# Six latent heads' roots in pairs: one 16-column chain per even/odd pair, and side work offered at each even query tile

## The chip, the cores and the metric

One core of one Trainium2 chip runs the whole program as a single launch. The metric is the device time of that launch in microseconds (us); the time of a kernel is the median over its runs.

## The reference, cut to what matters

The program is a two-layer encoder trunk over 512 tokens of width 1024. In each layer three groups of heads read one normalised input: six latent-attention heads (A), six dilated-window heads (B) and a state-space group (C). Their outputs are normalised, concatenated, projected and added to the stream; a gated, convolved MLP follows. The change touches group A alone:

```
q = split_heads(rmsnorm(c_q, q_gain) @ w_uq, MLA_HEADS)            # 6 heads of 96
kv = split_heads(rmsnorm(c_kv, kv_gain) @ w_ukv, MLA_HEADS)
k_nope, v = jnp.split(kv, [MLA_NOPE], axis=-1)
q = rmsnorm(q, qk_gain[0])
k = rmsnorm(jnp.concatenate([k_nope, k_rope], axis=-1), qk_gain[1])
```

followed by rotary embedding and dense attention over all 512 keys, in blocks of 128 queries. What matters here are the two root-mean-square norms per head and token: one reciprocal root for each query row and one for each key row.

## The kernel before, in words

Everything is held transposed: features on partitions, 512 tokens along the free axis. Large products run as three fp32r matmuls (high part by high, low by high, high by low: `mm3`, lines 381 to 383). `mixing(l, ...)` is one layer's attention half. Its attention stage is a loop over six turns, `TURNS = (b,0) (b,1) (a,0) (b,2) (a,1) (a,2)`, each a pair of heads of group B or A. A turn has two halves of two query tiles; each query tile has one `unit` per head of the pair:

- the scores (line 1170 for B, `mm3` for A) into one of three `sc` banks;
- on VectorE (DVE) line 1117, which scales them, takes the row minimum and writes `P`. For an A head the scale is a column of `qs`, the root of the query row;
- on ScalarE (ACT) line 1119, the exponential with row sums;
- four transposes of `P` on TensorE (PE), line 1123, and a copy out on DVE or ACT (1127, 1129).

After each half, `pv` (line 1141, 16 matmuls) adds the half's part of the output. `finish_pair` at the end of a turn takes the reciprocals of the sums (`rc`, line 1149), spreads them through `bx` (411) and four transposes (415), copies the result to `rb` (1152) and multiplies (1153).

The next heads are made beside the units, by the generator `side(n)`, stepped once after each half. It calls `next_qk(h)` and so `mla_qk(h, wq)` for head 0 at the end of turn 0, head 1 in turn 1, heads 2, 3, 4 and 5 in turns 2, 3, 3 and 4. An even call also makes the raw keys of heads h and h+1 (`kps`, `kraw[0]`, `kraw[1]`). Each call appends `roots` to the list `later`:

- `roots` of an even head sums squares by matmul into `ssh` (lines 1202, 1204), 12 columns: 4 for its queries, 8 for the keys of both heads. Two DVE operations finish `hv` (1206, 1207); `rsqrt` (lines 389 to 398, nine DVE operations, each reading the one before) takes the roots; then `qs` (1210) and `rks` (1213), the key roots of both heads.
- `roots` of an odd head does the same for the 4 query columns of its own.
- Each `roots` appends a `rest`: `bcast4` (four PE transposes, line 405) spreads the key roots, DVE line 1219 multiplies the raw key into `kf`, a tile named `glg` that has one buffer, and `qk_parts` splits it with a cast on ACT (913) and a subtraction on GpSimd (POOL, 914). The same `glg` is a scratch tile of the B heads' rotary step (922, 923).

`catch_up()` runs what stands in `later` at that moment; what it appends waits for the next call. It is called after `pv` of each half, after the step of `side`, and at the end of a turn. The order of each engine's instructions is fixed when the program is built, from program order, dependences and the offsets in `PRI` (`cu` 10, `qk` 20, `fin` 20 stand later; `glu` earlier). Each engine then runs its own list strictly in order. Of eight PSUM banks in this stage three hold scores, two transposes, one `pv`, and two (`ps`) everything else: `qps`, `kps`, `ssh`, the broadcasts, the GLU and value products, in turn.

Of the kernel before, what the change touches and what calls it, by code (L numbers as in the profile page):

```python
# [29 lines left out]
SETS = {("b", 0): 0, ("b", 1): 1, ("b", 2): 0, ("a", 0): 2, ("a", 1): 3, ("a", 2): 1, ("a", 3): 2, ("a", 4): 3, ("a", 5): 0}  # L30
# [194 lines left out]
def program(ctx, tc, a, out):  # L225
    nc = tc.nc
    V, S, T, G = nc.vector, nc.scalar, nc.tensor, nc.gpsimd
    mul, add, sub, mx_, mn_ = ALU.mult, ALU.add, ALU.subtract, ALU.max, ALU.min
# [21 lines left out]
    def tiny(name, n, dt=F32, bufs=2):  # L250
        return keep.tile([128, n], dt, tag=f"ty_{name}", name=name, bufs=bufs)

    def ht(i, dt=F32R):
        return hpool.tile([128, 512], dt, tag=f"t{i}", name=f"t{i}")
# [130 lines left out]
    def rsqrt(v, n, name):  # L385
        y = tiny("rs_y" + name, n)
        t = tiny("rs_t" + name, n)
        yi = y.bitcast(I32)
        V.tensor_scalar(yi, v.bitcast(I32), 1, None, op0=ALU.logical_shift_right)
        V.tensor_scalar(yi, yi, -1.0, float(0x5F3759DF), op0=mul, op1=add)  # L390

        V.tensor_tensor(t, y, y, mul)
        V.scalar_tensor_tensor(t, t, -0.1875, v, mul, mul)
        V.scalar_tensor_tensor(y, t, 0.5625, y, add, mul)
        V.tensor_tensor(t, y, y, mul)
        V.scalar_tensor_tensor(t, t, 64.0 / 9.0, v, mul, mul)
        V.scalar_tensor_tensor(t, t, -10.0 / 3.0, t, add, mul)
        cur["rs"] = V.scalar_tensor_tensor(y, t, 5.0, y, add, mul).ins
        return y

    def bcast4(r):

        o = ps("bc")
        for t in range(r.shape[1]):
            cur["pe"] = T.transpose(o[:, t * 128:(t + 1) * 128], r[:, t:t + 1].to_broadcast([128, 128]), ident).ins
        return o
# [387 lines left out]
    def mixing(l, background):  # L794
# [111 lines left out]
        def qk_parts(name, src, n):  # L906

            if n in (1, 2):
                i = 4 + 4 * n + 2 * (name == "k")
                hi, lo = ht(i), ht(i + 1)  # L910
            else:
                hi, lo = ((ap if n else mp).tile([128, N], F32R, tag=f"{name}{x}{n}", name=name + x) for x in "hl")
            S.copy(hi, src)
            G.tensor_tensor(lo, src, as32(hi), sub)
            return hi, lo
# [84 lines left out]
        for t in range(4):  # L1000
            c = slice(t * 128, t * 128 + 128)
# [11 lines left out]
        two = lambda t: t.unsqueeze(2).to_broadcast([128, 4, 2])  # L1013
        pairs = lambda t: t[:, 4:12].rearrange("p (t h) -> p t h", h=2)
        V.tensor_scalar(pairs(extra), two(so4[:, 1]), EPS, None, op0=add)
        ra = mp.tile([128, 8], F32, name="ra")
# [28 lines left out]
        kraw = [ht(6 + i, F32) for i in range(2)]  # L1045
# [4 lines left out]
        b = bcast4(ri)  # L1050
# [27 lines left out]
        later = []  # L1078

        def catch_up():  # L1080
            for _ in range(len(later)):
                with low("cu"):
                    later.pop(0)()
# [29 lines left out]
        def unit(S_ps, scale, qt, hh, PT, sums, pre):  # L1113

            P = ap.tile([128, N], F32, tag="P", name="P", bufs=3)
            nb = tiny("nb", 1, bufs=4)
            V.tensor_tensor_reduce(out=P, in0=S_ps, in1=zero if pre is None else pre, scale=scale, scalar=3e38,  # L1117
                                   op0=add, op1=mn_, accum_out=nb)
            S.activation(P, P, AF.Exp, scale=-1.0, bias=nb, accum_out=sums)  # L1119
            t_ps = ps("pt", "pt")  # L1120
            for kt_ in range(4):
                c = slice(kt_ * 128, kt_ * 128 + 128)
                T.transpose(t_ps[:, c], P[:, c], ident)  # L1123
            t3 = t_ps.rearrange("p (k q) -> p k q", k=4)
            dst = PT[:, :, qt % 2 * 128:qt % 2 * 128 + 128]
            if hh:
                V.tensor_copy(dst, t3)
            else:
                S.copy(dst, t3)
# [40 lines left out]
                        e = T.matmul(o[hh], x[r, c], y[r], start=i == 0, stop=i == 2).ins  # L1170
            return o

        rks = [None]

        def mla_qk(h, wq):
            odd = h % 2
            q_ps = ps("qps")
            c0, c1 = (slice(i * 256 + odd * 128, i * 256 + odd * 128 + 128) for i in range(2))
            mm3(q_ps, (wq[0][:, c0], wq[1][:, c0]), cq0, True, False)
            T.matmul(q_ps, wq[0][:, c1], cq1, start=False, stop=False)  # L1180
            T.matmul(q_ps, wq[1][:64, c1], cq1[:64], start=False, stop=True)
            if not odd:
                k_ps = ps("kps")
                c = slice(h * 64, h * 64 + 128)
                mm3(k_ps, (wuk[0][:, c], wuk[1][:, c]), ckv, True, True)
            sqq = sq_of(q_ps[:96], "sqq", 96)
            if not odd:
                sqk = sq_of(k_ps, "sqk")
                for i in range(2):
                    r = slice(i * 64, i * 64 + 64)  # L1190
                    S.activation(kraw[i][:64], k_ps[r], AF.Identity, scale=col(l, "gkn")[r])
            qf = tmp("glv")
            V.scalar_tensor_tensor(qf, q_ps, col(l, "gq"), tabA, mul, mul)
            q = qk_parts("q", qf, SETS["a", h])
            made = [q, None, None]

            def roots():
                n = 4 if odd else 12
                so = ps("ssh")
                for t in range(4):  # L1200
                    c = slice(t * 128, t * 128 + 128)
                    T.matmul(so[:, t:t + 1], sqq[:96, c], ssv[:96, 5:6], start=(t == 0), stop=bool(odd and t == 3))
                    if not odd:
                        T.matmul(so[:, 4 + 2 * t:6 + 2 * t], sqk[:, c], ssv[:, 10:12], start=False, stop=(t == 3))
                v = tiny("hv", 12)[:, :n]
                V.tensor_tensor(v, so[:, :n], ra2[:, :n], mul)
                V.tensor_tensor(v, v, extra[:, :n], add)
                r = rsqrt(v, n, "h")
                qs = made[2] = tiny("qs", 4, bufs=3)
                V.scalar_tensor_tensor(qs, r[:, 0:4], -(96.0 ** -0.5), ra[:, 0:4], mul, mul)  # L1210
                if not odd:
                    rks[0] = tiny("rks", 8)
                    V.tensor_tensor(rks[0].rearrange("p (h t) -> p t h", t=4), pairs(r), two(ra[:, 4:8]), mul)
                rk = rks[0][:, 4 * odd:4 * odd + 4]

                def rest():
                    b = bcast4(rk)
                    kf = tmp("glg")
                    V.tensor_tensor(kf, kraw[odd], b, mul)
                    made[1] = qk_parts("k", kf, SETS["a", h])  # L1220

                later.append(rest)

            later.append(roots)
            return made

# [71 lines left out]
        for n in range(6):  # L1298
            group, pr = TURNS[n]
            sums = ap.tile([128, 8], F32, tag="sums", name="sums", bufs=2)  # L1300
            o = ps("pv", "pv")
            beside = side(n)
            for half in range(2):
                PT = pt_tiles()
                for qt in (2 * half, 2 * half + 1):
                    if group == "b":
                        S2 = scores2(*ahead["b", pr], qt)
                    for hh in range(2):
                        if group == "b":
                            args = S2[hh], -0.125, K("bias", 384 - 128 * qt, 512)  # L1310
                        else:
                            q, k, qs = ahead["a", 2 * pr + hh]
                            args = scores(q, k, qt), qs[:, qt:qt + 1], None
                        unit(*args[:2], qt, hh, PT[hh], sums[:, hh * 4 + qt:hh * 4 + qt + 1], args[2])
                if group == "a":
                    background(2)
                with low("pv"):
                    pv(o[:, half * 256:half * 256 + 256], PT, dv if group == "b" else va[0], pr, half == 0, half == 1)
                catch_up()
                next(beside)  # L1320
                catch_up()
            catch_up()
            dst = ob if group == "b" else oa
            dst[pr] = ap.tile([128, N], F32, tag=f"ob{n % 4}", name=f"o{group}{pr}")
            with low("fin"):
                finish_pair(o, sums, dst[pr])
# [27 lines left out]
        for m in range(KD):  # L1354
            r = raw_tile(a["w_out"][l, m, :, :640], 640)
# [10 lines left out]
        for m in range(KD):  # L1366
            r = raw_tile(a["w_out"][l, m, :, 640:], 384)
# [175 lines left out]
    for l in range(L):  # L1543
        mod = lambda i, j0, j1: [lambda j=j: mod_chunk(i, j) for j in range(j0, j1)]
        first = l == 0
        later = bg(mod(0, 16, 40) if first else [])
# [25 lines left out]
```

## Time and profile before

| | us |
|---|---|
| median of 3 runs | 1496.19 |
| lowest, highest | 1490.89, 1500.64 |
| the profiled execution: its own time | 1495.62 |
| its span, first to last instruction | 1493.8 |

The profiled execution lies 0.57 us under the median. In the profile a busy engine is one that executes; PE is matmul, PEld its weight loads. The attention stage runs from about 186 to 348 us in layer 0 and from about 926 to 1082 us in layer 1.

### The profile page before, as it was taken

What the parts mean: (1) busy time and instruction counts of PE and PEld (TensorE: products, weight loads), DVE (VectorE), ACT (ScalarE), POOL (GpSimd) and SP (SyncE); (2) the same over time, 40 slices, a digit from 0 to 9 for tenths busy, and PEclk for the clock granted to TensorE, in tenths of its full rate; (3) what the DMA queues carried; (4) which work ended last, traced back from release to release, by engine and by line L of the source; (5) the groups of instructions that cost most, each with busy time, mean ns of one, the idle gap of its engine ahead of it and who ended that gap; (6) DMA issues with size and microseconds to landing.
All of it is one profiled execution on the core that took longest, in us unless ns stands there. A gap on an engine that the chain in (4) does not pass through costs nothing.

```text
span 1493.8 us, 20332 instructions
## 1 busy us (share of the span) xinstructions
PE 1383.6 (93%) x7260; PEld 1115.8 (75%) x7260; DVE 1014.5 (68%) x2062; ACT 685.9 (46%) x1336; POOL 343.7 (23%) x290
## 2 busy tenths in 40 slices
PE   6989778889899999999998989889899999999998
PEld 3668646568778878887888777666798888888886
DVE  6687867866698688688646487676657653654562
ACT  4464154654354433533446433666445432442441
POOL 1274312332212152242224443232210000000000
PEclk9899878999999999999999998999999999999999
DMA  7746223103747377467336441100042333323322
GB/s 264 243 139 207 94 58 118 60 10 101 213 159 246 106 233 269 130 225 241 108 101 194 118 141 57 33 18 10 10 131 66 94 96 99 99 88 96 99 90 94
DMA packets 79398, 185.11 MB, mean 124 GB/s; under 512 B 12864, under 2 KB 38208, under 8 KB 79296
## 3 DMA queue, kind: packets, MB, share of 16 engines
q1 hardware_dynamic: 77856, 181.37, 38.3%
q10 hardware_dynamic: 1440, 2.44, 0.5%
q8 instruction: 57, 0.93, 0.3%
q14 instruction: 45, 0.37, 0.1%
HBM read 165.95 MB, written 15.73 MB: 122 GB/s over the span
## 4 chain that ended last, share of the span: by engine, by line
PE 68%; DVE 15%; DMA 5%; ACT 5%; POOL 3%; issue 3%; SPq 1%; ACTq 0%; DVEq 0%; POOLq 0%
PE up L383 10%; PE up L382 10%; PE up L381 10%; PE dn L383 5%; PE dn L382 5%; PE dn L381 5%; PE pv L1141 3%; PE pt L1123 2%; DMA rawm<-in_wmod 2%; PE u L383 2%; PE u L382 2%; PE u L381 2%; DVE rawm L331 1%; DVE wl L376 1%; PE ssq L424 1%
## 5 line engine op out<-in xcount | busy, mean ns | idle before, releaser
L375 ACT CAST wh<-raw 128x512 fp32r<-128x512 f32 (+3 forms) x400 | 222.9, 567 | 325.5 <-PE dn L383 125.5
L376 DVE TENSOR_TENSOR wl<-raw,wh 128x512 fp32r<-128x512 f32 (+3 forms) x312 | 210.7, 679 | 128.8 <-ACT wh L375 128.4
L381 PE MATMUL up<-t,wh 128*128 128x512 f32 (+1 forms) x736 | 279.4, 381 | 2.5 <-ACT t L475 2.2
L382 PE MATMUL up<-t,wl 128*128 128x512 f32 (+1 forms) x736 | 279.0, 380 | 1.5 <-DVE wl L376 1.5
L383 PE MATMUL up<-t,wh 128*128 128x512 f32 (+1 forms) x736 | 278.1, 381 | 1.0 <-DVE t L476 1.0
L376 POOL TENSOR_TENSOR wl<-raw,wh 128x384 fp32r<-128x384 f32 (+1 forms) x88 | 111.8, 1274 | 232.5 <-ACT wh L375 211.4
L381 PEld LDWEIGHTS up<-t,wh 128*128 128x128 f32 x736 | 138.3, 188 | 29.8 <-ACT t L475 3.7
L382 PEld LDWEIGHTS up<-t,wl 128*128 128x128 f32 x736 | 138.2, 188 | 29.2 <-DVE wl L376 2.9
L383 PEld LDWEIGHTS up<-t,wh 128*128 128x128 f32 x736 | 137.2, 188 | 28.7 <-DVE t L476 2.0
L382 PE MATMUL dn<-gh,wl 128*128 128x512 f32 (+1 forms) x366 | 142.3, 391 | 1.6 <-DVE wl L376 1.6
L381 PE MATMUL dn<-gh,wh 128*128 128x512 f32 (+1 forms) x366 | 142.4, 391 | 0.0
L383 PE MATMUL dn<-gl,wh 128*128 128x512 f32 (+1 forms) x366 | 142.3, 390 | 0.0
L331 DVE CUSTOM_DVE_ANT_0 rawm<-rawm,cact,cols 128x1024 f32<-128x1024 f32 x68 | 94.2, 1388 | 19.6 <-DMA rawm<-in_wmod 19.4
L381 PE MATMUL u<-t,wh 128*128 128x512 f32 (+1 forms) x248 | 96.9, 399 | 6.7 <-ACT wh L375 3.8
L382 PE MATMUL u<-t,wl 128*128 128x512 f32 (+1 forms) x248 | 98.5, 398 | 1.4 <-POOL wl L376 0.9
L383 PE MATMUL u<-t,wh 128*128 128x512 f32 (+1 forms) x248 | 95.7, 391 | 2.6 <-DVE t L476 2.6
L382 PEld LDWEIGHTS dn<-gh,wl 128*128 128x128 f32 x366 | 68.8, 188 | 17.5 <-DVE wl L376 2.4
L381 PEld LDWEIGHTS dn<-gh,wh 128*128 128x128 f32 x366 | 68.8, 188 | 15.8 <-ACT gh L1462 0.7
L383 PEld LDWEIGHTS dn<-gl,wh 128*128 128x128 f32 x366 | 68.5, 188 | 15.5 <-DVE gl L1463 0.8
L1123 PE MATMUL pt<-cst,P 128*128 128x128 f32 x384 | 64.1, 295 | 15.3 <-ACT P L1119 13.7
L1119 ACT ACTIVATE P<-P,nb 128x512 f32<-128x512 f32 x96 | 68.9, 719 | 15.7 <-DVE nb L1117 11.7
L1446 DVE SCALAR_TENSOR_TENSOR zv<-up,cols,zv 128x511 f32<-128x511 f32 x44 | 32.9, 748 | 60.8 <-ACT zv L1445 60.6
(442 smaller groups left out, 2721.5 us busy)
## 6 DMA issues: line engine op xcount, KB each, us to landing
raw<-in_w_up SPq DMA_DIRECT2D x88, 512.0 KB, 3.7
rawm<-in_wmod SPq DMA_DIRECT2D x68, 512.0 KB, 4.4
raw<-in_w_dn SPq DMA_DIRECT2D x32, 448.0 KB, 3.3
rawm<-in_wquad SPq DMA_DIRECT2D x16, 512.0 KB, 6.1
raw<-in_w_dn SPq DMA_DIRECT2D x16, 512.0 KB, 3.6
raw<-in_w_in SPq DMA_DIRECT2D x40, 192.0 KB, 2.7
raw<-in_wmod SPq DMA_DIRECT2D x12, 512.0 KB, 3.6
raw<-in_w_in SPq DMA_DIRECT2D x16, 320.0 KB, 3.3
```

What stands on the lines that cost most here:

```text
L331: V.tensor_tensor_reduce(out=r, in0=r, in1=cact, scale=1.0, scalar=col(l, "bmod", j), op0=mul, op1=add, accum_out=modv[l][:, j:j + 1])
L375: S.copy(hi[:, :n], src)
L376: (eng or V).tensor_tensor(lo[:, :n], src, as32(hi[:, :n]), sub)
L381: T.matmul(o, wh, xh, start=first, stop=False)
L382: T.matmul(o, wl, xh, start=False, stop=False)
L383: return T.matmul(o, wh, xl, start=False, stop=last).ins
L424: cur["pe"] = T.matmul(o[:, t:t + 1], s[:, t * 128:(t + 1) * 128], w, start=(t == 0 and i == 0), stop=(t == nt - 1 and i == len(parts) - 1 ...
L1119: S.activation(P, P, AF.Exp, scale=-1.0, bias=nb, accum_out=sums)
L1123: T.transpose(t_ps[:, c], P[:, c], ident)
L1141: T.matmul(o[hh * 64:hh * 64 + 64], v[:, k, c0:c0 + 64], PT[hh][:, k], start=(first and k == 0), stop=(last and k == 3))
L1446: V.scalar_tensor_tensor(z[:, 1:], o[:, :N - 1], col(l, "cw0", j), z[:, 1:], mul, add)
```

## The change

`roots` of an even head stops after `hv`: it fills columns 0 to 11 of a 16-column tile. `roots` of the odd head fills columns 12 to 15, takes one `rsqrt` over all 16, makes `qs` of both heads and `rks`, and appends two `rest` calls, for the even and for the odd head. A further `catch_up()` stands after the units of query tiles 0 and 2. The tile `qs` has four buffers instead of three.

```diff
@@ -1170,7 +1170,7 @@
-        rks = [None]
+        two_of = []
 
         def mla_qk(h, wq):
@@ -1193,6 +1193,10 @@
             made = [q, None, None]
+            if not odd:
+                two_of[:] = [], tiny("hv", 16)
+            heads, hv = two_of
+            heads.append(made)
 
             def roots():
                 n = 4 if odd else 12
@@ -1202,24 +1206,25 @@
-                v = tiny("hv", 12)[:, :n]
+                v = hv[:, 12:16] if odd else hv[:, :12]
                 V.tensor_tensor(v, so[:, :n], ra2[:, :n], mul)
                 V.tensor_tensor(v, v, extra[:, :n], add)
-                r = rsqrt(v, n, "h")
-                qs = made[2] = tiny("qs", 4, bufs=3)
-                V.scalar_tensor_tensor(qs, r[:, 0:4], -(96.0 ** -0.5), ra[:, 0:4], mul, mul)
                 if not odd:
-                    rks[0] = tiny("rks", 8)
-                    V.tensor_tensor(rks[0].rearrange("p (h t) -> p t h", t=4), pairs(r), two(ra[:, 4:8]), mul)
-                rk = rks[0][:, 4 * odd:4 * odd + 4]
-
-                def rest():
-                    b = bcast4(rk)
+                    return
+                r = rsqrt(hv, 16, "h")
+                for m, c in zip(heads, (0, 12)):
+                    m[2] = tiny("qs", 4, bufs=4)
+                    V.scalar_tensor_tensor(m[2], r[:, c:c + 4], -(96.0 ** -0.5), ra[:, 0:4], mul, mul)
+                rks = tiny("rks", 8)
+                V.tensor_tensor(rks.rearrange("p (h t) -> p t h", t=4), pairs(r), two(ra[:, 4:8]), mul)
+
+                def rest(i):
+                    b = bcast4(rks[:, 4 * i:4 * i + 4])
                     kf = tmp("glg")
-                    V.tensor_tensor(kf, kraw[odd], b, mul)
-                    made[1] = qk_parts("k", kf, SETS["a", h])
-
-                later.append(rest)
+                    V.tensor_tensor(kf, kraw[i], b, mul)
+                    heads[i][1] = qk_parts("k", kf, SETS["a", h - 1 + i])
+
+                later.extend([lambda: rest(0), lambda: rest(1)])
 
             later.append(roots)
@@ -1312,6 +1317,8 @@
                         unit(*args[:2], qt, hh, PT[hh], sums[:, hh * 4 + qt:hh * 4 + qt + 1], args[2])
+                    if qt % 2 == 0:
+                        catch_up()
                 if group == "a":
                     background(2)
```

## Rows read from the trace of the kernel before

**Rows 1.** The page: busy time by engine, and the chain that ended last.

```profile
PE 1383.6 (93%) x7260; PEld 1115.8 (75%) x7260; DVE 1014.5 (68%) x2062; ACT 685.9 (46%) x1336; POOL 343.7 (23%) x290
...
PE 68%; DVE 15%; DMA 5%; ACT 5%; POOL 3%; issue 3%; SPq 1%; ACTq 0%; DVEq 0%; POOLq 0%
```

**Rows 2.** Busy time by stretch: length, five engines' busy us (count), clock, DMA.

```profile
186.00:348.00 162.00, 132.72 (x760) 90.91 (x760) 117.81 (x302) 94.63 (x200) 45.36 (x32) 0.88 0.19 57
926.00:1082.00 156.00, 139.66 (x876) 99.64 (x876) 107.64 (x291) 98.66 (x210) 40.18 (x31) 0.96 0.07 20
228.00:240.00 12.00, 8.20 (x39) 5.97 (x39) 8.84 (x28) 4.86 (x12) 1.28 (x1) 0.62 0.22 75
...
258.00:270.00 12.00, 7.53 (x24) 4.45 (x23) 10.04 (x24) 3.55 (x7) 6.52 (x4) 0.72 0.40 125
...
279.00:291.00 12.00, 11.31 (x83) 7.65 (x81) 11.90 (x41) 9.22 (x22) 3.69 (x3) 1.00 0.37 111
```

**Rows 3.** Timeline of DVE, layer 0: the chain of head 0 (start, us).

```profile
228.97 0.17 DVE L1206 TENSOR_TENSOR hv<-ssh,ra 128x12 f32<-128x12 f32 x1 [2.29 <-PE ssh L1204]
...
230.94 0.16 DVE L389 TENSOR_SCALAR rs_yh<-hv 128x12 int32<-128x12 int32 x1
...
234.37 0.19 DVE L1149 RECIPROCAL rc<-sums 128x8 f32<-128x8 f32 x1
...
237.34 0.17 DVE L1213 TENSOR_TENSOR rks<-rs_yh,ra 128x8 f32<-128x8 f32 x1
```

**Rows 4.** Timeline of DVE: chain of head 3 (layer 0) and head 2 (layer 1).

```profile
303.54 0.17 DVE L389 TENSOR_SCALAR rs_yh<-hv 128x4 int32<-128x4 int32 x1
...
305.32 0.16 DVE L1210 SCALAR_TENSOR_TENSOR qs<-rs_yh,ra 128x4 f32<-128x4 f32 x1
...
1001.30 1.17 DVE L397 SCALAR_TENSOR_TENSOR rs_th<-rs_th 128x12 f32<-128x12 f32 x1
```

**Rows 5.** Timeline of PE: the broadcast of head 0's key roots, both layers.

```profile
237.56 1.12 PE L405 MATMUL bc<-cst,rks 128*128 128x128 f32 x4 [1.35 <-DVE rks L1213]
238.47 1.06 PE L415 MATMUL bc<-cst,bx 128*128 128x128 f32 x4
239.46 0.79 PE L381 MATMUL gv<-ych,wh 128*128 128x512 f32 x1
...
961.87 1.12 PE L405 MATMUL bc<-cst,rks 128*128 128x128 f32 x4 [0.19 <-DVE rks L1213]
```

**Rows 6.** Timeline of PE, layer 0: sums for `mc`, and two odd heads' queries.

```profile
287.42 0.95 PE L424 MATMUL ssq<-wmc,sqk 128*128 128x1 f32 x8
...
297.57 0.47 PE L381 MATMUL qps<-t,smh 128*128 128x512 f32 x1 [0.72 <-DVE rb L1099]
...
320.98 0.50 PE L381 MATMUL qps<-t,smh 128*128 128x512 f32 x1 [0.30 <-DVE glg L1219]
```

**Rows 7.** Timeline of DVE, layer 0: first units of A turns, and a key.

```profile
253.96 0.74 DVE L1117 CUSTOM_DVE_ANT_0 P<-sc,zcol,qs 128x512 f32<-128x512 f32 x1
...
266.10 0.74 DVE L1117 CUSTOM_DVE_ANT_0 P<-sc,zcol,qs 128x512 f32<-128x512 f32 x1
...
294.06 0.74 DVE L1117 CUSTOM_DVE_ANT_0 P<-sc,zcol,qs 128x512 f32<-128x512 f32 x1
...
305.67 0.69 DVE L1219 TENSOR_TENSOR glg<-t,bc 128x512 f32<-128x512 f32 x1 [0.19 <-PE bc L405]
...
308.96 0.75 DVE L1117 CUSTOM_DVE_ANT_0 P<-sc,zcol,qs 128x512 f32<-128x512 f32 x1 [0.48 <-PE sc L383]
...
334.62 0.75 DVE L1117 CUSTOM_DVE_ANT_0 P<-sc,zcol,qs 128x512 f32<-128x512 f32 x1 [0.27 <-PE sc L383]
```

**Rows 8.** Timeline of DVE, layer 1: head 1's key and the tile's next writer.

```profile
979.91 0.69 DVE L1219 TENSOR_TENSOR glg<-t,bc 128x512 f32<-128x512 f32 x1
...
982.76 0.73 DVE L922 STREAM_SHUFFLE glg<-dr 128x512 f32<-128x512 f32 x1
```

**Rows 9.** Timeline of POOL, layer 1: the low part of head 1's key.

```profile
981.33 1.29 POOL L914 TENSOR_TENSOR kl<-glg,kh 128x512 fp32r<-128x512 f32 x1 [2.15 <-ACT kh L913]
```

## The prediction

> **What bounds the kernel now.** I read the page first. PE is busy 93% of the span and holds 68% of the chain that ended last [rows 1]; most of that is MLP and projection work that the change does not touch. So the second view is busy time by stretch, over the two attention stages: PE is idle 162.00 - 132.72 = 29.3 us in layer 0 and 156.00 - 139.66 = 16.3 us in layer 1 [rows 2]. What the change can win lies in these 45.6 us, plus what PE loses at a low granted clock (mean 0.88 and 0.96 there). The third view is the timeline of each engine. What the reader should see there: the units of a B turn wait for no new head and run early, whereas the units of an A turn wait for heads made beside them. In layer 0 the first A unit starts at 253.96, the one that waits for head 1 at 266.10; in the next A turn one unit runs at 294.06 and the next only at 308.96 [rows 7]. In those holes the side work is the path: squares, roots, key, scores, through two `ps` banks and five in-order engines. Both edits act on that side path and on nothing else.
>
> **Part 1: what is removed.** A pair of heads now costs DVE 13 small operations for the even head (two for `hv`, nine of `rsqrt`, `qs`, `rks`) and 12 for the odd: 25. After it they are 2 + 2 + 9 + 2 + 1 = 16. Nine go per pair, 54 in six pairs, so DVE should show 2008 instructions instead of 2062 [rows 1]. Width costs next to nothing: 0.17 us at 4 columns and 0.16 to 0.17 at 12 [rows 3, 4]; I take 16 columns as the same. Alone, nine take 305.32 - 303.54 = 1.8 us, 0.2 each [rows 4]. Between wide operations a chain is stretched instead: head 0's, from `hv` to `rks`, lasts 237.34 - 228.97 = 8.4 us [rows 3], mostly the wide work between. DVE time as such (54 x 0.2 = 11 us at most) is worth little, since DVE is 73% busy in layer 0's stage (117.81 of 162, [rows 2]); what counts is who stands behind the chain.
>
> Removing the even chain also removes the even `rest` from its place: four transposes, `kf`, a cast and a POOL subtraction go behind the odd chain. No DMA is among them. I go through the three hand-overs of a layer.
>
> *Heads 0 and 1 (A).* In layer 0 PE reaches the transposes of head 0's key roots before the chain is done, waits 1.35 us and runs them for 1.12 us; behind it stands `finish_pair`'s broadcast at 238.47, and behind that the GLU at 239.46 [rows 5]. The broadcast's own input hangs on `rc`, at 234.37 [rows 3]. Gone, the broadcast could start at best 238.47 - 234.56 = 3.9 us earlier, at worst none. An ACT copy lies between, so I take 3.5, the nearest row being that of `rc`. The clock here is 0.62 [rows 2]; a shorter hole gives back some of that, for which I add 0.6, between 0 and half of the busy time at 228 to 240 (4.1). In layer 1 the wait is only 0.19 [rows 5]: I take 1.0, from 0 to the 1.12 plus 0.19 shown. Together 5.1.
>
> *Heads 2 and 3 (B).* In layer 0 the even chain falls where DVE is full, 11.90 of 12 us, and PE nearly so, 11.31 [rows 2]. PE alone gives 0.7 us there. But head 3's queries start only at 297.57, behind the `mc` broadcast's bank, and that side chain starts with the sums at 287.42 that PE takes together with head 2's key broadcast [rows 6]. An earlier start moves the hole at 294.06 to 308.96. Bounds: nothing to the 8.4 us of a stretched chain. I take 2, nearer to PE's own idle time; 1 in layer 1, whose stage has about half the idle time. Together 3.
>
> *Heads 4 and 5 (C).* Head 5's queries at 320.98 wait for head 4's `kf` [rows 6]. `kf` (0.69, as [rows 7]) and its broadcast (at the most 1.12, [rows 5]) leave that place: 0 to 1.8; I take 1 in each layer, since PE then has other work. Together 2.
>
> Saved: 5.1 + 3 + 2 = 10.1 us.
>
> [...] The operation of head 2's chain at 1001.30 took 1.17 us instead of 0.17 [rows 4]. [...] By the rows alone such an operation is merely long. [...]
>
> **Part 2: what is added.** Both keys now hang on the odd chain. Before, only the odd head's query roots did, because the even chain had made the key roots of both. After a chain ends, a key takes from `kf` at 305.67 to its unit at 308.96, 3.3 us [rows 7]. And the two keys cannot overlap: `kf` has one buffer, `glg`. In layer 1 `kf` starts at 979.91, its POOL reader runs from 981.33 to 982.62, and the next writer of the tile starts at 982.76 [rows 8, 9]. So the second `kf` starts 2.85 us after the first. Behind it in DVE's list stand the units and the B heads' rotary step, which uses the same tile.
>
> In B this reads: head 2's first unit moves from 294.06 to about 308.96, where head 3's was, and head 3's to 308.96 + 2.85 = 311.8. In C the second head's unit at 334.62 [rows 7] moves likewise, less what that chain gains from an earlier start. The cost of one hand-over is at least 0, if the first head's units of two query tiles, value products and next queries fill PE; at most 2.85 plus a unit that nothing covers, for which I take the 0.75 of line 1117 [rows 7] and the 0.50 of one 512-column product [rows 6] as the part that does not overlap: 4.1 us. I take half of 2.85, 1.42, since the first head's two tiles can fill one half: 6 x 1.42 = 8.5 us in two layers.
>
> **Part 3: the added `catch_up`.** In nine of the twelve half turns of a layer nothing stands in the list there. It matters in turns 1, 3 and 4, where it offers both `rest` calls before `pv` instead of behind it. No instruction is added. Alone it is worth 0 while the odd chain ends later than the units beside it, as it does at 305.32 where the hole began after 294.06 [rows 4, 7]; it may gain the time of a `pv`, or lose it if PE then waits at the transposes. I take 0.
>
> **The sum.** -10.1 + 8.5 = -1.6 us, made against the profiled execution's 1495.62 (span 1493.8, 1.8 around it): 1494.0. The median is 0.57 above that execution, so 1494.6; I write 1494.5.
>
> **The rivals.**
>
> *The keys come too late (slower).* Mechanism: at each of six hand-overs PE runs dry between odd chain and first score. Place: before the first unit of turns 2, 4 and 5. Price: 4.1 us each, 24.6, less 10.1 saved: +14.5, 1510. It decides from the point where PE has no value products, `pv` or queries left, that is from a cost above 1.7 us per hand-over (10.1 / 6). For it: PE is busy only 7.53 of 12 us at 258 to 270 already, clock 0.72 [rows 2], just where both keys will be awaited. Against: 266.10 waited for head 1 before too. [...]
>
> *The side chain was the limit (faster).* If the two `ps` banks, held through a stretched even chain, set the pace of the side path, each even chain gone brings all behind it forward. With 8.4 us of one stretched chain [rows 3] and a third of six of them exposed: 16.8, less a cost of 0.5 per hand-over (3): -13.8, 1482. For it: 15 us without a unit at 294 to 309. Against: PE works through most of that.
>
> *It does not do what it says.* The fixed order is made anew at build, and DVE's 54 operations were filler: 1496.
>
> **How the numbers follow.** Forecast (within about 6 us of 1494.5) 0.52; too late 0.20; side chain 0.20; no effect 0.08. A measurement of this kernel can tell about 1%, 15 us, from no change. Of the faster rival a little over half lies beyond 1% (under 1481.2): 0.12. Of the slower one half lies beyond (over 1511.2): 0.10. The rest, 0.78, is within. The range reaches to 1481 and 1509, which leaves out those tails and a little of the slower rival.
>
> **What would show it.** Right: 2008 DVE instructions; `rsqrt` rows 16 wide, six per line instead of twelve; no wait of PE at line 405 ahead of the first GLU product; the second `kf` of a pair about 2.9 us behind the first; no A unit before the odd chain's end. Wrong: stage lengths that differ by more than 5 us from 162 and 156; PE idle in the stages falling by over 10 us (side chain) or rising by over 10 (late keys).

## The result, and the profile after

The changed kernel takes 1510.51 us (median of 4 runs, 1507.45 to 1511.50), the kernel before 1493.54 beside it: a ratio of 1.0102, 95% interval 1.0077 to 1.0128, so 15 us slower by the ratio and 17 by the medians. I had forecast 1494.5 in a range of 1481 to 1509. The time lies 1.5 us outside that range, with the other sign, and within 0.5 us of the first rival, "The keys come too late".

The page after. The first line answers to [rows 1]: the 54 DVE operations are gone as counted (2008), and PE is busy for 12.9 us more, although it runs as many matmuls as before. The second line is the chain that ended last, in which PE's share has grown.

```profile
PE 1396.5 (93%) x7260; PEld 1127.9 (75%) x7260; DVE 1004.7 (67%) x2008; ACT 686.2 (45%) x1336; POOL 341.1 (23%) x290
...
PE 73%; DVE 13%; ACT 4%; DMA 4%; POOL 3%; issue 2%; SPq 1%; ACTq 0%; POOLq 0%; DVEq 0%
```

Busy time by stretch, with the columns of [rows 2]. First the two attention stages of the kernel before, each measured from the start of its first unit on line 1117 to the start of its last `rc`:

```profile
189.69:348.30 158.61, 129.33 (x743) 89.07 (x742) 116.11 (x300) 92.58 (x198) 45.36 (x32) 0.88 0.19 58
930.79:1068.47 137.68, 121.52 (x740) 84.76 (x738) 98.30 (x267) 89.50 (x193) 40.18 (x31) 0.95 0.06 18
```

Then the changed kernel: the same two stages; two stretches of [rows 2]; and two that hold the hand-over to turn 5 in each layer.

```profile
189.57:354.49 164.92, 132.59 (x743) 92.50 (x742) 113.01 (x273) 92.56 (x198) 43.48 (x32) 0.87 0.18 56
937.30:1084.76 147.46, 127.44 (x740) 88.33 (x738) 92.86 (x241) 89.45 (x193) 40.21 (x31) 0.90 0.05 17
...
228.00:240.00 12.00, 11.27 (x68) 8.34 (x69) 9.12 (x18) 6.85 (x16) 1.29 (x1) 1.00 0.21 69
258.00:270.00 12.00, 10.18 (x49) 8.15 (x47) 9.19 (x18) 6.37 (x16) 5.76 (x5) 0.85 0.24 72
...
328.00:340.00 12.00, 8.00 (x41) 5.41 (x42) 6.86 (x20) 3.64 (x8) 3.94 (x4) 0.72 0.00 0
1058.00:1070.00 12.00, 8.37 (x40) 5.54 (x41) 6.67 (x18) 3.66 (x7) 3.78 (x4) 0.62 0.00 1
```

The hole at 228 to 240 is closed: PE is busy 11.27 of 12 us at a granted clock of 1.00, where [rows 2] has 8.20 at 0.62. New holes stand before turn 5. There PE is busy two thirds of the time, at a mean granted clock of 0.72 and 0.62; in steps of 2 us it lies between 0.50 and 1.00 there.

The stages place the loss. In layer 0 the stage takes 158.6 us before and 164.9 after, in layer 1 137.7 and 147.5. Together they go from 296.3 to 312.4: 16.1 us. What is left of the span is 1197.5 before and 1197.3 after. In these two executions the whole loss lies in the two stages.

It has two parts. PE is idle for 6.9 us more (29.3 to 32.3 us in layer 0, 16.2 to 20.0 in layer 1). And it is busy for 9.2 us more with the same matmuls (743 and 740), at mean clocks of 0.87 and 0.90 instead of 0.88 and 0.95.

The view of PE's waits names the idle part. The columns are us in total, times, longest. First the kernel before, layer 0's stage and then layer 1's:

```profile
PE bc L405 <- DVE rks L1213: 1.4, 1, 1.4
...
PE bc L405 <- DVE rks L1213: 0.2, 1, 0.2
```

Then the changed kernel, in the same order:

```profile
PE bc L405 <- DVE rks L1219: 5.3, 3, 2.9
...
PE bc L405 <- DVE rks L1219: 4.1, 2, 2.2
```

PE waits 9.4 us at the key broadcast for the key roots, against 1.6 before. What stands around such a wait is seen in the two timelines of layer 0's last hand-over (that its pair costs nothing when it is merged alone is found further down). DVE in the changed kernel:

```profile
325.71 0.16 DVE L1210 TENSOR_TENSOR hv<-ssh,ra 128x4 f32<-128x4 f32 x1 [0.28 <-PE ssh L1206]
...
326.96 0.87 DVE L1211 TENSOR_TENSOR hv<-hv,extra 128x4 f32<-128x4 f32 x1
327.86 1.21 DVE L389 TENSOR_SCALAR rs_yh<-hv 128x16 int32<-128x16 int32 x1
329.11 1.19 DVE L390 TENSOR_SCALAR rs_yh<-rs_yh 128x16 int32<-128x16 int32 x1
...
331.94 0.17 DVE L1219 TENSOR_TENSOR rks<-rs_yh,ra 128x8 f32<-128x8 f32 x1
...
333.96 0.69 DVE L1224 TENSOR_TENSOR glg<-t,bc 128x512 f32<-128x512 f32 x1 [1.25 <-PE bc L405]
336.68 0.69 DVE L1224 TENSOR_TENSOR glg<-t,bc 128x512 f32<-128x512 f32 x1 [2.03 <-POOL kl L914]
...
339.11 0.75 DVE L1117 CUSTOM_DVE_ANT_0 P<-sc,zcol,qs 128x512 f32<-128x512 f32 x1 [0.64 <-PE sc L383]
```

PE in the same stretch:

```profile
329.23 0.66 PE L1123 MATMUL pt<-cst,P 128*128 128x128 f32 x4 [2.98 <-ACT P L1119]
...
332.17 1.97 PE L405 MATMUL bc<-cst,rks 128*128 128x128 f32 x8 [2.28 <-DVE rks L1219]
334.07 3.23 PE L1141 MATMUL pv<-pt,va 128*64 128x256 f32 x16
```

The chain ends at 331.94. From there the broadcast, `kf`, cast, subtraction and scores follow one after the other, and the first unit of turn 5 starts 7.2 us later, at 339.11 (331.51 before). PE is not idle in these 7.2 us: it is busy for 6.91 of them, with `pv` and the sums for the next mix between broadcast and scores, at a mean clock of 0.67. It idles 2.98 and 2.28 us ahead of that, with 0.66 us of transposes between, and the 16 products of `pv` then take 3.23 us, at a mean clock of 0.59. At a clock of 1.00 the same 16 take 1.95 (before, at 325.82):

```profile
325.82 1.95 PE L1141 MATMUL pv<-pt,va 128*64 128x256 f32 x16
```

### The profile page after: what moved, and what is told of

Same layout as the page of the kernel before. It is cut to its first block, busy times and chain, and to the rows that moved or that the text cites. A ratio compares the mean times of both kernels' runs of the same rounds, so it can differ in the third digit from the quotient of the medians.

```text
span 1509.7 us, 20260 instructions
## 1 busy us (share of the span) xinstructions
PE 1396.5 (93%) x7260; PEld 1127.9 (75%) x7260; DVE 1004.7 (67%) x2008; ACT 686.2 (45%) x1336; POOL 341.1 (23%) x290
## 4 chain that ended last, share of the span: by engine, by line
PE 73%; DVE 13%; ACT 4%; DMA 4%; POOL 3%; issue 2%; SPq 1%; ACTq 0%; POOLq 0%; DVEq 0%
PE up L381 10%; PE up L383 10%; PE up L382 10%; PE dn L383 5%; PE dn L382 5%; PE dn L381 5%; PE pv L1141 3%; PE pt L1123 2%; PE u L382 2%; PE u L383 2%; PE u L381 2%; PE wo L382 2%; PE wo L381 2%; PE wo L383 2%; PE sc L1170 1%
```

## The experiments

Theories. K: both keys hang on the merged chain, and so come late. M: the added mid-half call puts key broadcasts ahead of `pv`. G: the two keys take turns in `glg`. Later Q: the even head's query roots come late. In the table, the ratio is against the kernel before, run beside each (its median there was 1493.96 us for e1 to e4, 1495.74 for e5 to e8, 1494.44 for e9 to e11, 1495.85 for e12); "stages" is the sum of the two stage lengths and "rest" what is left of the span, both of the profiled execution; "wait" is PE at line 405 for `rks` in both stages.

| kernel | median us | ratio (95% interval) | stages | rest | wait |
|---|---|---|---|---|---|
| before | 1493.54 | 1 | 296.3 | 1197.5 | 1.6 |
| changed | 1510.51 | 1.0102 (1.0077 to 1.0128) | 312.4 | 1197.3 | 9.4 |
| e1, no mid-half call | 1513.29 | 1.0130 (1.0105 to 1.0155) | 315.9 | 1194.8 | 9.4 |
| e2, before with the call | 1500.39 | 1.0045 (1.0024 to 1.0066) | 296.4 | 1202.4 | 1.7 |
| e3, second key in `glv` | 1504.97 | 1.0075 (1.0050 to 1.0099) | 304.5 | 1197.2 | 8.4 |
| e4, two chains | 1496.42 | 1.0015 (0.9996 to 1.0034) | 300.2 | 1196.7 | 0 |
| e5, late queries only | 1496.13 | 1.0008 (0.9986 to 1.0031) | 297.4 | 1198.7 | 0 |
| e6, late keys only | 1513.78 | 1.0134 (1.0109 to 1.0158) | 311.8 | 1197.8 | 11.3 |
| e7, merge of heads 0, 1 | 1504.93 | 1.0071 (1.0042 to 1.0100) | 305.9 | 1200.1 | 5.5 |
| e8, of heads 4, 5 | 1493.93 | 0.9990 (0.9972 to 1.0008) | 294.5 | 1198.1 | 1.4 |
| e9, of heads 2, 3 | 1503.04 | 1.0052 (1.0034 to 1.0070) | 297.2 | 1206.9 | 0.4 |
| e10, e8 and `glv` | 1491.79 | 0.9985 (0.9966 to 1.0004) | 290.0 | 1197.5 | 2.0 |
| e11, before, heads 4, 5 merged, `glv` | 1498.68 | 1.0023 (1.0006 to 1.0040) | 306.2 | 1194.1 | 3.8 |
| e12, of heads 2 to 5 | 1499.22 | 1.0023 (1.0005 to 1.0042) | 301.6 | 1194.4 | 4.3 |

**e1 and e2: the mid-half call.** In e1 it is taken out of the changed kernel, in e2 it is put into the kernel before:

```diff
-                    if qt % 2 == 0:
-                        catch_up()
```

> The changed kernel without the added mid-half call. Theory K (late keys: both keys and both query roots of a pair hang on the one merged chain behind the odd head): the loss stays, 1507 to 1511 us. Rival M (the added call is what costs: it offers the key broadcasts, which wait for rks, to PE ahead of the half's value products, as seen where bc at 332.17 waits 2.28 us and pv at 334.07 stands behind it): the time falls back by half of the loss or more, to about 1495 to 1502. Rival G (the two keys take turns in one buffer of glg): the loss stays too, as by K.

> The kernel before with nothing but the added mid-half call. K and G: as before, 1490 to 1497 us, since the chains and the keys are as they were. M: slower by half of the loss or more, 1502 to 1510, with pv standing behind a key broadcast at the turns in which a rest is in the list (three turns of a layer).

Without the call the changed kernel is no faster (1513.29), and PE waits for `rks` as long as with it. M is not the cause. The time is even 2 us above K's range. In the kernel before the call alone costs 6.4 us, which lies between the two forecasts. The attention stages do not have it: their sum is 296.4, as before, and the wait for `rks` is 1.7. In the profiled execution the loss comes outside the stages: what stands behind layer 1's takes 431.7 us instead of 425.3. There PE waits 2.63 us for a product of the last mix that no key has a part in. PE in e2:

```profile
1085.24 0.36 PE L381 MATMUL wo<-mb,wh 128*128 128x256 f32 x1 [2.63 <-DVE rb L1099]
```

For the 20 us around it the clock is 0.91. Busy time by stretch in e2:

```profile
1077.11:1097.11 20.00, 16.90 (x129) 16.56 (x130) 8.99 (x24) 4.87 (x11) 0.00 (x0) 0.91 0.20 60
```

**e3: the second key in another tile.**

```diff
-                    kf = tmp("glg")
+                    kf = tmp(("glg", "glv")[i])
```

> The changed kernel with the second key of a pair written to another tile (glv in place of glg), so that the second kf need not wait for the first one's subtraction. G: six hand-overs gain 1.3 to 2.7 us each, 8 to 16 in all, so 1495 to 1503 us, and the second kf stands at most 1.3 us behind the first instead of 2.7 to 2.9. K and M: the second head is not what PE waits for; 1507 to 1511, and the first units of turns 2, 4 and 5 start where they did.

It gains 5.5 us and ends between the two forecasts. The second `kf` now follows the first after 0.60 us instead of 3.41 (layer 0, heads 0 and 1), but both still wait for the chain. DVE in e3:

```profile
248.37 0.17 DVE L1219 TENSOR_TENSOR rks<-rs_yh,ra 128x8 f32<-128x8 f32 x1
250.20 0.68 DVE L1224 TENSOR_TENSOR glg<-t,bc 128x512 f32<-128x512 f32 x1
250.80 0.68 DVE L1224 TENSOR_TENSOR glv<-t,bc 128x512 f32<-128x512 f32 x1
255.50 0.75 DVE L1117 CUSTOM_DVE_ANT_0 P<-sc,zcol,qs 128x512 f32<-128x512 f32 x1 [0.84 <-PE sc L383]
```

G is a part: a third of the loss by the medians, half of it by the stages of one profiled execution each (304.5 against 312.4). Most of it is won at the last hand-over of layer 0, where the first unit of turn 5 stands 149.5 us behind the stage's start in the changed kernel and 142.2 in e3 (132.1 and 129.7 in layer 1). The first unit of turn 2 in layer 0 stands where it did (66.9 and 66.8).

**e4: the merge alone undone.** The even head takes its own chain of 12 columns again, the odd head one of 4. Both `rest` calls stay behind the odd roots, and the mid-half call stays.

```diff
+                r = rsqrt(v, n, "h")
...
                 if not odd:
+                    rks[0] = tiny("rks", 8)
...
                     return
-                r = rsqrt(hv, 16, "h")
```

> The changed kernel with the merge alone undone: the even head's chain of 12 columns makes its query roots and both heads' key roots, the odd head's chain of 4 its query roots, as before; both keys are still made behind the odd head's roots, and the mid-half call stays. If the lateness of rks itself is the cost (K, narrow form), the time falls to 1493 to 1499 us and DVE shows about 2062 operations again. If the cost is that the first head's key is put behind the odd head's roots in the order, or M, or G, it stays at 1506 to 1511, although the even chain is back.

1496.42: the 54 operations are back, and 14.1 us are gone. PE has no wait for `rks` left in either stage. The timeline shows where the time was. DVE in e4, layer 0, heads 0 and 1:

```profile
237.40 0.17 DVE L1219 TENSOR_TENSOR rks<-rs_yh,ra 128x8 f32<-128x8 f32 x1
...
247.10 0.67 DVE L1226 TENSOR_TENSOR glg<-t,bc 128x512 f32<-128x512 f32 x1
250.22 0.69 DVE L1226 TENSOR_TENSOR glg<-t,bc 128x512 f32<-128x512 f32 x1
250.90 0.74 DVE L1117 CUSTOM_DVE_ANT_0 P<-sc,zcol,qs 128x512 f32<-128x512 f32 x1
256.79 0.16 DVE L1216 SCALAR_TENSOR_TENSOR qs<-rs_yh,ra 128x4 f32<-128x4 f32 x1
257.10 0.75 DVE L1117 CUSTOM_DVE_ANT_0 P<-sc,zcol,qs 128x512 f32<-128x512 f32 x1
```

Both keys are made before the odd head's chain ends (its `hv` starts at 243.08, its `qs` at 256.79), and 0.3 us behind that `qs` the odd head's unit runs. In the changed kernel the same chain ends earlier, at 250.64, and the same two units run later, at 256.47 and 262.72: the merge brought the chain's end forward, and put the making of two keys behind it. DVE in the changed kernel:

```profile
250.64 0.17 DVE L1219 TENSOR_TENSOR rks<-rs_yh,ra 128x8 f32<-128x8 f32 x1
252.20 0.69 DVE L1224 TENSOR_TENSOR glg<-t,bc 128x512 f32<-128x512 f32 x1 [0.20 <-PE bc L405]
255.61 0.69 DVE L1224 TENSOR_TENSOR glg<-t,bc 128x512 f32<-128x512 f32 x1 [1.17 <-POOL t L914]
256.47 0.75 DVE L1117 CUSTOM_DVE_ANT_0 P<-sc,zcol,qs 128x512 f32<-128x512 f32 x1 [0.17 <-PE sc L383]
262.72 0.75 DVE L1117 CUSTOM_DVE_ANT_0 P<-sc,zcol,qs 128x512 f32<-128x512 f32 x1 [0.90 <-PE sc L383]
```

The clock has a share in that: over the changed kernel's `pv` at 244.39 it is 0.52, and the 16 products take 3.59 us, against 1.95 in e4. In e4 PE runs the key broadcast between the squares and turn 1's `pv`; in the changed kernel it idles there, and waits for the roots behind `pv`. PE in e4, then in the changed kernel:

```profile
242.91 1.26 PE L405 MATMUL bc<-cst,rks 128*128 128x128 f32 x8
244.10 1.95 PE L1141 MATMUL pv<-pt,vb 128*64 128x256 f32 x16
```

```profile
244.39 3.59 PE L1141 MATMUL pv<-pt,vb 128*64 128x256 f32 x16 [0.85 <-DVE pt L1127]
250.86 1.52 PE L405 MATMUL bc<-cst,rks 128*128 128x128 f32 x8 [2.88 <-DVE rks L1219]
```

From the chain's end to the first unit PE is busy for 4.53 of 5.83 us, with value products and scores, at a clock of 0.56. e4 has a clock of 1.00 from 247 to 257. Busy time by stretch, changed kernel, then e4:

```profile
250.64:256.47 5.83, 4.53 (x15) 3.32 (x16) 4.03 (x10) 1.33 (x3) 1.96 (x1) 0.56 0.77 207
```

```profile
247.00:257.00 10.00, 6.97 (x36) 5.36 (x36) 9.90 (x23) 4.97 (x10) 3.32 (x4) 1.00 0.52 155
```

**e5 and e6: which roots must be early.** Both have two chains like e4, cut at other columns. In e5 the first takes the 8 key columns and the second all 8 query columns:

```diff
                 if not odd:
+                    r = rsqrt(hv[:, 8:16], 8, "h")
...
+                r = rsqrt(hv[:, 0:8], 8, "h")
```

In e6 the first takes the even head's 4 query columns and the second the other 12:

```diff
+                r = rsqrt(hv[:, 4:16], 12, "h") if odd else rsqrt(hv[:, 0:4], 4, "h")
```

> The two-chain kernel (e4) with the columns split otherwise: the even head's chain takes the 8 key columns of both heads, the odd head's chain the 8 query columns of both. Only the first head's query roots come late. If late key roots are the cost of the merge (K): as e4, 1494 to 1499 us. If the unit that waits for the even head's qs is the cost (Q): 1505 to 1511.

> The complement: the even head's chain takes its own 4 query columns, the odd head's chain the 8 key columns of both heads and its 4 query columns. Only the key roots come late; DVE has as many operations as in e4. K: as the changed kernel, 1506 to 1512 us, or a little more, since the chain saved by the merge is not saved here. Q: 1494 to 1499.

Early keys with late queries: 1496.13. Late keys with early queries: 1513.78, with 11.3 us of wait. The two differ in which columns go first and in little else (the second chain is 12 wide, not 8). K holds, and Q falls.

**e7, e8, e9 and e12: one pair at a time.** In e4, the merge put back for some pairs, `h // 2` being 0, 2, 1, or over 0:

```diff
+                if h // 2 == 0:
+                    if not odd:
+                        return
+                    r = rsqrt(hv, 16, "h")
```

> The two-chain kernel (e4, 1496.4 us) with the merge for heads 0 and 1 alone. By the changed kernel's trace the hand-over to turn 2 gained 1.5 us in layer 0 and lost 4.4 in layer 1: K prices it at +3, 1497 to 1502 us. If the loss is spread evenly over the three pairs, +4.7: 1501. If only the last pair costs (nothing of PE's work is left there but turn 4's units), the merge of pair 0 gains the chain that it saves: 1491 to 1496.

> The two-chain kernel (e4, 1496.4 us) with the merge for heads 4 and 5 alone. By the changed kernel's trace the hand-over to turn 5 lost 6 us in layer 0 and 5 in layer 1, so K prices it at +11: 1505 to 1510 us. If the loss is spread evenly over the three pairs, +4.7: 1501. If C is not the place, 1494 to 1499.

> The two-chain kernel (e4, 1496.4 us) with the merge for heads 2 and 3 alone. If the prices of the three pairs add up to the changed kernel's loss (14.1 over e4; pair 0 took 8.5, pair 2 gave 2.5): +8, 1502 to 1507 us. If they don't add, because pair 2 costs only behind a pair that is late already: +2 or +3, 1497 to 1500, as the 1.5 us that the changed kernel's turn 3 lost in layer 0 and the 1 us in layer 1 say.

> The two-chain kernel (e4, 1496.4 us) with the merge for heads 2 to 5, heads 0 and 1 alone taken in two chains. If the prices add up (pair 1 alone 6.6, pair 2 alone -2.5): 1500 to 1502 us, and the changed kernel's 1510.5 less pair 0's 8.5 says the same, 1502. If pair 2 is free only behind an early pair 1: 1505 to 1510. If pair 1's price was no more than the order it happened to get: 1494 to 1498.

My reading of the places from the trace was wrong twice: heads 0 and 1 cost more than K, an even spread or a cost at the last pair alone had said (8.5 us; 11.3 on top of the other two, 1510.51 - 1499.22), heads 4 and 5 nothing (K had said 1505 to 1510). Heads 2 and 3 cost what was left over, 6.6, as the first forecast of e9 said. By the ratios, which allow for the kernel before of each batch, heads 0 and 1 cost 8.4 us, heads 2 and 3 5.5 and heads 4 and 5 -3.7, each with 4 to 5 us either way. e12 came out between its forecasts (1499.22, where 1500 to 1502 and 1494 to 1498 were given); in ratios it is what its parts add up to (1.0052 + 0.9990 - 1.0015 = 1.0027, measured 1.0023). All three pairs sum to 0.9990 + 1.0052 + 1.0071 - 2 x 1.0015 = 1.0083, against 1.0102 measured, with intervals of 0.002 to 0.003 on each. The rows offer a reason why the last pair is free. DVE in e4, layer 0, heads 4 and 5:

```profile
325.89 0.16 DVE L1216 SCALAR_TENSOR_TENSOR qs<-rs_yh,ra 128x4 f32<-128x4 f32 x1
325.96 0.68 DVE L1226 TENSOR_TENSOR glg<-t,bc 128x512 f32<-128x512 f32 x1
```

There the fixed order puts the first key behind the odd head's `qs` even with `rks` early (319.29), so there is no overlap for a merge to take away (in layer 1 likewise, at 1048.38 and 1048.46). Alone at that place (e8) the broadcast waits 0.71 us, not 2.28. Merged behind heads 2 and 3 the last pair costs nothing either (e12 against e9). Whether it does behind a late pair of heads 0 and 1, as in the changed kernel, no run shows. PE in e8:

```profile
321.30 1.09 PE L405 MATMUL bc<-cst,rks 128*128 128x128 f32 x8 [0.71 <-DVE rks L1227]
```

The price of heads 2 and 3 is not placed. In e9's profile, the slowest of its ten executions, the stages are no longer than in e4 (297.2 against 300.2), and 10 us more than in e4 stand outside them, among others in the same wait for the last mix as in e2 (2.83 us, PE in e9):

```profile
1087.49 0.35 PE L381 MATMUL wo<-mb,wh 128*128 128x256 f32 x1 [2.83 <-DVE rb L1099]
```

**e10 and e11: is there a faster version?** e10 is e8 with e3's edit. e11 is the kernel before with heads 4 and 5 merged, and e3's edit; of its code behind `hv`:

```diff
+                if h // 2 == 2:
+                    if not odd:
+                        return
+                    r = rsqrt(hv, 16, "h")
...
-                later.extend([lambda: rest(0), lambda: rest(1)])
+                later.extend([lambda: rest(0), lambda: rest(1)] if h == 5 else [lambda: rest(odd)])
```

> The kernel that merges heads 4 and 5 alone (e8, 1493.9 us) with the second key of each pair in the other tile, as in e3. If G is worth there what it was in the changed kernel (5.5): 1487 to 1490 us. If the second key is not what PE waits for once the chains of the first two pairs are early: 1492 to 1496.

> The kernel before (no mid-half call, each key of heads 0 to 3 made right behind its own head's roots) with the merge for heads 4 and 5 alone, and odd keys in the other tile. Before's keys of a pair lie far apart, so the tile gives little: K expects what e8 gained over e4 and a little more, 1489 to 1494 us. If the merge of pair 2 needs the mid-half call to be free: 1497 to 1502.

e10 has the shortest stages of all (290.0 in its profiled execution), but its median is 1491.79 and the interval of its ratio reaches 1.0004: not told apart from the kernel before. e11 is slower, as much as its second forecast said; whether for the reason given there, the missing call, no run isolates. The trace has another: in the kernel before head 4's `kf` ran at 320.23, ten us ahead of head 5's `qs`; there a merge does take an overlap away.

## Why the prediction was wrong

**Part 1, the operations and the shorter chain: right in kind.** DVE shows 2008 operations and the chain rows are 16 wide. The chain did end earlier where it could: 250.64 against 256.79 in e4.

**Part 1, head pairs 0 and 1 (5.1 us): the hole closed, but not by the merge.** PE's stretch at 228 to 240 went to 11.27 us at a clock of 1.00, 3.1 us more. But e4, which has the even chain, shows the same there. Busy time by stretch in e4:

```profile
228.00:240.00 12.00, 11.27 (x66) 8.23 (x66) 10.38 (x30) 6.85 (x14) 1.30 (x1) 1.00 0.23 67
```

e2, where head 0's `rest` stands where it did before, keeps the hole (8.20 us):

```profile
228.00:240.00 12.00, 8.20 (x32) 5.77 (x30) 9.63 (x29) 5.03 (x11) 1.64 (x2) 0.57 0.23 67
```

So what closes it is that this `rest` is offered behind the odd roots, out of the way of `finish_pair`. I had counted it as a gain of joining the chains, and moving the `rest` alone brings it. No run shows time won by it: e4, with the hole closed, is not told apart from the kernel before (1.0015, 0.9996 to 1.0034).

**Part 1, pairs 2/3 and 4/5 (3 and 2 us): not seen.** In the changed kernel turn 4's last unit starts at 326.29 instead of 317.19, and head 5's `hv` at 325.71 instead of 325.92: no earlier.

**Part 2, the keys (1.42 us per hand-over, 8.5 in all): the step that failed.** I named the mechanism, both keys behind the odd chain, and sized it by the lag of the second `kf` alone, halved. That lag came as worked out (2.7 to 3.4 us), and e3 prices it at 5.5 us, near to the 8.5. Two things had no term. The first is the wait for the key roots themselves: Part 1 took it as gone with the even broadcast (1.35 us in layer 0, 0.19 in layer 1), but it went behind the odd chain and grew to 9.4 us. The second is the clock around such waits, which my sum has only as a gain of 0.6 us: more than half of the stages' 16.1 us is PE's busy time for the same matmuls (9.2), not its idle time (6.9). Of the way from `rks` to the first unit, 5.8 us at turn 2 and 7.2 at turn 5 in layer 0, I had named the 3.3 us from `kf` to unit in [rows 7] and priced nothing, since other work could fill PE. PE did have work there (4.53 of 5.83 us, and 6.91 of 7.17), but at clocks of 0.56 and 0.67. With Part 1's saving unseen, the merge costs 14.1 us net (changed kernel against e4), where my terms for it gave a gain of 1.6. No run parts the saving from the cost, since the merge moves both.

**Part 3, the call, taken at 0.** Within the change the medians give it 2.8 us (e1 against the changed kernel), but the intervals of the two ratios overlap. In the kernel before it costs 6.4. In neither does PE wait longer for `rks` with it (9.4 and 9.4, 1.7 and 1.6).

**The rival** had the direction and the late keys right. That its total (1510) lies within 0.5 us is luck: it was 24.6 us of cost less 10.1 saved, and the runs show 14.1 net and no saving. It spread the price evenly, 4.1 us on six hand-overs; the runs put most of it on the first pair of each layer and none on the last pair merged alone. Nor does PE run dry between chain and first score: it waits ahead of the broadcast (2.88 us at 250.86, 2.28 at 332.17) and is then busy at a low clock (0.56 and 0.67). The sign that I set for late keys, PE's idle time in the stages rising by over 10 us, did not come (6.9); the stage lengths did show it (6.3 and 9.8 us).

**The long operations of the chain.** Long operations like the one of [rows 4] are there too: of head 5's chain, shown above, those at 326.96, 327.86 and 329.11 end at 327.83, 329.07 and 330.30, each within 0.04 us of the end of a POOL operation. POOL in the changed kernel:

```profile
326.55 1.26 POOL L1092 TENSOR_TENSOR sqk<-sqk,sqq 128x512 f32<-128x512 f32 x1 [5.81 <-ACT sqq L878]
327.76 1.27 POOL L914 TENSOR_TENSOR ql<-glv,qh 128x512 fp32r<-128x512 f32 x1
328.99 1.27 POOL L1092 TENSOR_TENSOR sqk<-sqk,sqq 128x512 f32<-128x512 f32 x1
```

Together they add 2.8 us (0.87 + 1.21 + 1.19 less three times 0.17) to a chain that PE was waiting for. They are no difference between the two kernels, though: the kernel before has them in the same head's chain (1.12 us at 326.92 and 1.18 at 328.86, each ending within 0.02 us of a POOL operation). The one of [rows 4] ends 0.03 us from such an end. The rows show that the ends fall together, not why: no run took these POOL operations away.

## What to carry to other kernels

Before two chains are joined, look at what is made between the end of the first and the end of the second: here two keys were, and the join put them behind both. Fifty-four operations saved on an engine with idle time weighed nothing against that. If chains must be joined or cut anew, let the results with the longest way still to go (keys: broadcast, multiply, split, score) leave first and those used last (a scale at the unit) leave late; e5 and e6, with the same count of operations, lie 17.7 us apart on little else. And price a wait of PE together with the products behind it: here the idle time rose by 6.9 us and the busy time, for the same matmuls, by 9.2.

## What was not expected

Parts of the program that no edit touches took different times: the time outside the two attention stages was 1194.1 to 1206.9 us over the fourteen profiled executions. How much of that is the order made anew, and how much the spread between executions of one kernel (the kernel before took 1488.4 to 1503.6 us in one batch), these profiles do not show. One idle stretch of 2.6 to 2.8 us of PE behind layer 1's stage, within 20 us at a clock of 0.91 in e2, is in both kernels with the largest rest (e2 and e9); four others (e4, e5, e7, e8) have it at 0.9 us. A verdict on a part that costs 5 us or less needs the stage lengths beside the total, and one profiled execution of each does not settle it.
